# A hybrid encoder block on one core: the first norm applied by diagonal matmuls in a fixed TensorE order, and the mixer's first half in another order

## The chip, the core and the metric

The kernel runs on one core of a Trainium2 chip. A core has TensorE (PE in the profile; its weight loads are PEld), VectorE (DVE), ScalarE (ACT), GpSimd (POOL) and SyncE (SP, which only issues DMAs). The metric is the device time of one execution in microseconds. A comparison takes several runs of both kernels on the same chip; one more execution is recorded by the hardware profiler.

## The reference

x is 1024 tokens by 1024 features, float32. One trunk layer is computed:

```python
x = x + 0.5 * swiglu(rmsnorm(x, ffn1_norm), w_gate1, w_up1, w_down1)   # D_FF = 2816
h = rmsnorm(x, mix_norm); p = h @ w_in
u_a, v_a, qkv, z, b_raw, a_raw = split(p)
y_a = gelu(u_a) * (W_s @ layernorm(gelu(v_a)) + b_s)       # blocks of 128 tokens, 8 groups of 64 channels
q, k, v = split(silu(causal_conv4(qkv)))                   # 4 heads x 128; q, k are l2-normed
beta = sigmoid(b_raw); g = cumsum(-exp(a_log) * softplus(a_raw + dt_bias))   # within chunks of 64
L = strict(beta_i k_i.k_j exp(g_i - g_j))                  # per chunk
u, w = solve(I + L, [beta v, beta k exp(g)])
S, o = scan over the chunks (S: 128 x 128 per head), with attn = tril(q_i.k_j exp(g_i - g_j))
y_b = rmsnorm(o, dn_norm) * silu(z)
x = x + concat(y_a, y_b) @ w_out
x = x + 0.5 * swiglu(rmsnorm(x, ffn2_norm), w_gate2, w_up2, w_down2)
return rmsnorm(x, final_norm)
```

## The kernel before

**Arithmetic.** A large product of f32 data is made of three matmuls in the fp32r type: each operand is split into a high part (a cast by ScalarE) and a low part (a subtraction by VectorE or GpSimd), and `mm3` (L55) adds high x high, high x low and low x high in PSUM. The FFNs use a Winograd form of Strassen's scheme: the activations are cut into four blocks (two token halves by two feature halves), `Combos` holds the transposed blocks B11, B12, B21, B22 and their sums T1 to T4, `load_gu` (L181) makes the matching sums of the weights on GpSimd and splits them. Matmul outputs go to two pools of four PSUM banks, "mm" and "ax".

**Order.** The program is written with a tile framework. A planner puts the instructions of each engine in an order by their place in the program and its own estimate of when they are ready, so the order on an engine can differ from that of the text; at run time each engine goes through its list in order and waits by semaphores. Tiles of one tag share a fixed number of buffers, and a new tile waits until the last user of its buffer is done. DMAs are issued by the SP and ACT queues in their order.

**First FFN's start (`start1`, L467 to L500).** The 8 tiles of x (128 tokens each) arrive by SP; a broadcast copy of the gain (`grow`, L64) arrives by the ACT queue. `normed` (L80) squares and sums a tile on ScalarE, forms the reciprocal root (VectorE L76, then a power on GpSimd, L70), and multiplies x by root and gain on VectorE (L82; L493 for the second four tiles). `Combos.blocks` transposes each tile in 128 x 128 pieces on TensorE (L95), and ScalarE and VectorE evacuate them as split blocks (L118, L119, L141, L142) and as the sums' sources (L137, L148, L150). The first chunk of gate and up is computed plainly, 256 tokens of each half at a time (`gu_plain`, L229): 96 matmuls of 256 columns each time. Then `put_sums` makes T1 to T4, and from chunk 1 on (`gu`) the dense stream runs: 84 matmuls of 512 columns a chunk, while GpSimd and VectorE prepare the next chunk's weights and, every other chunk, the sums for the down product (`weight_sums`, `hidden_sums`).

**Mixer, first half (`middle`).** hT is the normed x, transposed. `token_steps` gives a token-major product, one step per 128 tokens (24 matmuls of 256 columns); `proj_steps` gives a feature-major one, 24 matmuls of 512 columns for each token half, then the convolution (ScalarE copy, four VectorE passes L871 and L873, SiLU on ScalarE L875). In the text the order is:

1. v0 (first half of v), and beside it `decay(h)` (L786) for the four heads: rows of g are broadcast from DRAM, VectorE and GpSimd form g_i - g_j with a mask, ScalarE exponentiates, twice: EL for L, EA for attn.
2. `keys(h, fill)` (L885): the projection of head h's keys, two steps of `fill` (z1, the second half of z), then for both token halves transposes, norms, k's decayed copies, the Gram matmuls in banks "sc" and "sd" and Lm, which goes to DRAM.
3. `substitute()` (L911): the 32 x 32 diagonal blocks of all L are inverted at once, 31 steps of two VectorE passes (L920, L922).
4. `gm_consts`, and v1 (second half of v): GELU, then `mix` (L1074, layernorm on VectorE with a power on GpSimd) and `spatial` (L1088, matmuls with W_s for a pair of tiles, bias added by VectorE).
5. Projections 8 and 0 (v and q of head 0), then per half head: `inverse` (TensorE and copies), `values`, `queries`, woven with the next projections, and `scan`, which walks four chunk pairs through three PSUM banks "sc", "sq", "sd".

## Time and profile before

| what | value |
|---|---|
| median of 3 runs | 1849.43 us (1847.9 to 1852.1) |
| the profiled execution | 1841.22 us |
| its span, first to last instruction | 1839.4 us |
| mean granted TensorE clock | 0.992 |
| from HBM, to HBM | 208.83 MB, 91.77 MB |
| up to the dense stream of the first FFN | 0 to 62.7 us |
| first FFN and z0 | 62.7 to 707 us |
| mixer, v0 to the first inverse | 707 to 893 us |
| mixer, inverse and scan | 893 to 1055 us |
| output projection, second FFN, final norm | 1055 to 1839 us |

How to read it: a row of a timeline is start, duration, engine, line, operation, out<-in by the program's names, shapes and count; in brackets stands the engine's idle time before it and what ended the wait. A row of groups gives count, busy time, mean ns of one, and idle time before. Line numbers are those of the kernel before.

### The profile page before, as it was taken

The page shows a single profiled execution, that of the slowest core. Times are in us where ns is not written, and L with a number is a line of the kernel's source. Part 1 is how long each engine was busy: PE and PEld are TensorE (multiplying, and loading weights), DVE is VectorE, ACT ScalarE, POOL GpSimd, SP SyncE. Part 2 cuts the span into 40 slices and gives each one's busy share as a digit, 9 for nine tenths or more (in the row PEclk, how much of TensorE's full clock was granted, in tenths as well). Part 3 has the DMA queues.
Part 4 walks back from the last instruction along what each step waited for, and adds up shares of the span by engine and source line. Part 5 has one row for each costly group of instructions (what it writes and reads, how often), then busy time and mean ns, then how long its engine had stood idle before and what let it go on. Part 6 is the DMA issues. An engine that isn't in the chain of part 4 may idle for free.

```text
span 1839.4 us, 25484 instructions
## 1 busy us (share of the span) xinstructions
PE 1784.1 (97%) x9735; PEld 1524.8 (83%) x9735; DVE 1191.7 (65%) x1531; ACT 686.6 (37%) x1193; POOL 747.9 (41%) x583
## 2 busy tenths in 40 slices
PE   5999999999999999898999999999999999999997
PEld 4888888888788889797788989988888888878886
DVE  6867676665565575769655344587776766656546
ACT  6333332333343454432344533452333323243433
POOL 4667666565140012212132420366666665614001
PEclk9999999999999999999999999999999999999999
DMA  5353443544957445453432254334535445495744
GB/s 196 108 175 136 162 152 134 184 158 163 339 188 258 155 177 164 140 195 100 133 94 67 90 197 136 109 104 165 178 132 171 144 154 188 142 344 185 264 142 149
DMA packets 134441, 302.26 MB, mean 164 GB/s; under 512 B 27408, under 2 KB 42032, under 8 KB 134320
## 3 DMA queue, kind: packets, MB, share of 16 engines
q1 hardware_dynamic: 131824, 296.20, 46.9%
q10 hardware_dynamic: 2496, 4.44, 0.8%
q8 instruction: 76, 1.25, 0.3%
q14 instruction: 45, 0.37, 0.1%
HBM read 208.83 MB, written 91.77 MB: 163 GB/s over the span
## 4 chain that ended last, share of the span: by engine, by line
PE 78%; DVE 8%; DMA 5%; POOL 4%; issue 3%; ACT 2%; SPq 0%; POOLq 0%; DVEq 0%; ACTq 0%
PE mm L53 43%; PE ax L53 32%; POOL s L191 1%; POOL t L278 1%; DMA left<-hq 1%; DVE acc L873 1%; PE ax L95 1%; PE sd L53 1%; DMA graw<-in_f1gu_dram 1%; POOL s L278 1%; PE sc L53 1%; DVE T L119 0%; DVE unit L62 0%; DVE wk L62 0%; DVE E L797 0%
## 5 line engine op out<-in xcount | busy, mean ns | idle before, releaser
L53 PE MATMUL mm<-unit 128*128 128x512 f32 x1056 | 244.9, 392 | 4.2 <-ACT unit L61 2.2
L53 PEld LDWEIGHTS mm<-unit 128*128 128x128 f32 x1056 | 198.8, 189 | 47.4 <-ACT unit L61 3.3
L191 POOL TENSOR_TENSOR s<-graw 128x512 f32<-128x512 f32 x84 | 130.3, 1551 | 262.9 <-DMA graw<-in_f2gu_dram 116.0
L62 DVE TENSOR_TENSOR ga<-graw,ga 128x512 fp32r<-128x512 f32 x134 | 155.9, 1166 | 99.9 <-ACT ga L61 99.2
L61 ACT CAST gs<-s 128x512 fp32r<-128x512 f32 x168 | 104.5, 622 | 301.8 <-PE mm L53 151.0
L62 DVE TENSOR_TENSOR unit<-left,unit 128x1024 fp32r<-128x1024 f32 x84 | 101.9, 1215 | 133.0 <-ACT unit L61 132.3
L53 PE MATMUL ax<-T,gs 128*128 128x512 f32 x792 | 183.1, 389 | 0.0
L53 PE MATMUL ax<-unit 128*128 128x512 f32 x792 | 180.5, 389 | 0.0
L53 PEld LDWEIGHTS ax<-T,gs 128*128 128x128 f32 x792 | 148.7, 188 | 30.8
L53 PEld LDWEIGHTS ax<-unit 128*128 128x128 f32 x792 | 148.7, 188 | 30.8
L62 DVE TENSOR_TENSOR gs<-s,gs 128x512 fp32r<-128x512 f32 x168 | 172.7, 1030 | 2.3
L53 PE MATMUL mm<-B,ga 128*128 128x512 f32 (+1 forms) x864 | 166.8, 347 | 3.3 <-ACT B L118 1.9
L61 ACT CAST unit<-left 128x1024 fp32r<-128x1024 f32 x84 | 82.5, 982 | 230.2 <-PE ax L53 100.5
L53 PE MATMUL mm<-T,gs 128*128 128x512 f32 x720 | 166.5, 389 | 0.0
L53 PEld LDWEIGHTS mm<-B,ga 128*128 128x128 f32 x864 | 139.5, 194 | 23.4 <-ACT B L118 2.5
L53 PEld LDWEIGHTS mm<-T,gs 128*128 128x128 f32 x720 | 135.2, 188 | 28.0
L70 POOL TENSOR_TENSOR rs<-rs,half 128x1 f32<-128x1 f32 (+1 forms) x29 | 19.2, 662 | 334.5 <-DVE rs L76 334.4
L53 PE MATMUL mm<-actT,wk 128*128 128x512 f32 x576 | 150.4, 403 | 0.0
L53 PE MATMUL ax<-B,ga 128*128 128x512 f32 x528 | 127.2, 390 | 1.4 <-DVE ga L62 1.4
L53 PE MATMUL mm<-wk,actT 128*128 128x256 f32 x960 | 123.5, 285 | 2.7 <-DVE wk L62 2.7
L53 PEld LDWEIGHTS mm<-wk,actT 128*128 128x128 f32 x960 | 117.4, 190 | 3.4 <-DVE wk L62 3.0
L53 PEld LDWEIGHTS mm<-actT,wk 128*128 128x128 f32 x576 | 103.6, 188 | 18.8
(239 smaller groups left out, 3046.0 us busy)
## 6 DMA issues: line engine op xcount, KB each, us to landing
left<-hq SPq DMA_DIRECT2D x70, 512.0 KB, 5.0
graw<-in_f1gu_dram SPq DMA_DIRECT2D x44, 512.0 KB, 5.4
wq<-t SPq DMA_DIRECT2D x44, 512.0 KB, 2.8
hq<-s SPq DMA_DIRECT2D x44, 512.0 KB, 3.1
graw<-in_f2gu_dram SPq DMA_DIRECT2D x44, 512.0 KB, 4.7
right<-wq SPq DMA_DIRECT2D x40, 512.0 KB, 4.8
wd<-in_f1wd_dram SPq DMA_DIRECT2D x22, 512.0 KB, 6.6
hq<-sg SPq DMA_DIRECT2D x22, 512.0 KB, 3.7
```

The lines of the kernel that those rows point to most:

```text
L53: nc.tensor.matmul(*args, **kw)
L61: nc.scalar.copy(h, src)
L62: nc.vector.tensor_tensor(l, src, h, op=ALU.subtract)
L70: nc.gpsimd.tensor_tensor(o, i, half[:, :w], op=ALU.pow)
L95: nc.tensor.transpose(ps[:, i * P:(i + 1) * P], blk(i), ident)
L191: nc.gpsimd.tensor_tensor(f, u, v, op=op)
L278: nc.gpsimd.tensor_tensor(o, u, v, op=op)
L873: nc.vector.scalar_tensor_tensor(acc, pad[:, j:j + 512], cw[:, blk, j:j + 1], acc, op0=ALU.mult, op1=ALU.add)
```

## The change

There are three groups of edits. The first is at the start: the gain arrives as a column layout (`f1g`, 128 x 8) and the norm is no longer applied to x. Instead a diagonal matrix of the tile's reciprocal roots is made (identity times root), and the block's transposition becomes a plain f32 matmul of x with that diagonal; the gain is applied on evacuation, per partition. Tiles 0, 1, 4, 5 come first, then 2, 3, 6, 7; four tiles fill a bank of 512 columns. TensorE's order is fixed by hand there, and begins with 24 matmuls of the identity. `gu_plain` becomes a generator that goes by k over all four accumulators (in both FFNs), woven with the blocks.

```diff
+        def scaled_blocks(self, i, pp, xts, dg, g, f, b12, ahead):
+            sl = slice(i * 256, i * 256 + 256)
+            t3, t1, t2, t4 = self.f[i] = f
+            def less(o, src, c, v):
+                nc.vector.scalar_tensor_tensor(o, src, g[:, c:c + 1], v, op0=ALU.mult, op1=ALU.subtract)
+            def put(h, l, src, c):
+                nc.scalar.mul(h, src, g[:, c:c + 1])
+                less(l, src, c, h)
...
+            def turn(k):
+                cs = range(len(banks), len(banks) + k)
+                banks.extend(bank(*pp) for _ in cs)
+                for n, x in enumerate(xts):
+                    for c in cs:
+                        mm(banks[c][:, n * P:n * P + P], x[:, c * P:c * P + P], dg[:, n * P:n * P + P], start=True, stop=True)
+            turn(ahead)
+            for c in range(8):
+                if c == len(banks):
+                    turn(1)
+                u, v = banks[c][:, :256], banks[c][:, 256:]
+                k = c % 4
+                if c < 4:
+                    b = self.block("B11")
+                    put(b[:, 0, k, sl], b[:, 1, k, sl], u, c)
+                    nc.scalar.mul(t3[:, k], u, g[:, c:c + 1])
+                    b = b12[k // 2]
+                    put(b[:, 0, k % 2], b[:, 1, k % 2], v, c)
+                    less(t1[:, k], v, c, t3[:, k])
+                else:
+                    b = self.block("B21")
+                    put(b[:, 0, k, sl], b[:, 1, k, sl], u, c)
+                    b = self.block("B22")
+                    put(b[:, 0, k, sl], b[:, 1, k, sl], v, c)
+                    less(t2[:, k], v, c, t1[:, k])
+                    less(t4[:, k], u, c, t2[:, k])
+                yield
...
+            def plain(i, dg, fs, b, ahead, also=()):
+                bl = cb.scaled_blocks(i, f.X, [xs[t] for t in order[i]], dg, g1, fs, b, ahead)
+                together(islice(bl, 4))
+                together(also)
+                pr = f.gu_plain(slice(i * 256, i * 256 + 256), b)
+                for _ in bl:
+                    next(pr)
+                together(pr)
+            with tc.manual_schedule(engines={mybir.EngineType.PE}):
+                warm = bank(*f.X)
+                for _ in range(24):
+                    mm(warm[:, :P], ident, ident, start=True, stop=True)
+                weights = f.load_gu(0, True)
+                dg = factors(order[0], nc.vector.tensor_scalar_mul)
+                together(islice(weights, 2))
+                xs.update(load_x(xdram, order[1]))
+                plain(0, dg, four(cb.sums() + cb.sums()), b12(), 4, weights)
+                dg = factors(order[1], nc.scalar.mul)
...
+                plain(1, dg, fs, b12(), 1)
+            together(f.load_gu(1), *(cb.scaled_sums(i, ("T2", "T1", "T3", "T4"), (V, G, V, G)) for i in range(2)))
```

`scaled_sums` is `put_sums` for 256 tokens at a time. The first `weight_sums` moves from chunk 1 to chunk 2. The reciprocal roots of norms, keys and `mix` are formed by two GpSimd instructions (`rsqrt`: add, power) in place of a VectorE and a GpSimd one. At the end of the second FFN the last tile's halves change places, and tile 6's last multiplication is handed back to the caller.

The second group is the decay: only EL stays in `decay`, g_i goes into the exponential as ScalarE's bias (four instructions of 128 columns in place of one of 512), and attn's factor is made in `values`, per half head:

```diff
     def decay(h):
-        EL[h], EA[h] = (xp.tile([P, 2, 512], F32, tag="x", name="E") for _ in range(2))
+        EL[h] = xp.tile([P, 2, 512], F32, tag="x", name="E")
         for hf in range(2):
...
+            rows_of(grb, h * 2 + hf)
+            (nc.vector if hf else nc.gpsimd).tensor_tensor(v4(EL[h][:, hf]), masked(K(C_ML)), v4(grb), op=ALU.subtract)
+            exponents(EL[h][:, hf], gc, h * 2 + hf)
...
             nc.scalar.copy(self.u, up)
+            aT = self.aT = big("aT", 2)
+            rows_of(aT, self.n)
+            nc.vector.tensor_tensor(v4(aT), masked(cma), v4(aT), op=ALU.add)
+            exponents(aT, ngc, self.n)
             yield
```

The third is the order of steps 2 to 5. v1 becomes the filling of the keys, z1 comes after them, TensorE's order is fixed from the keys to the end of z1, and projection 8's VectorE work is queued behind the last substitution step:

```diff
-    fill = token_steps([a["wz1"][0], a["wz1"][1]], 256, spill("z", 1), hT)
-    for h in range(HEADS):
-        keys(h, fill)
-    together(fill)
-    substitute()
     gm = gm_consts()
+    gm_shift(gm)
     later = []
-    tm("v", 1, ev_v(gm, later))
+    fill = steps("v", 1, ev_v(gm, later))
+    PE = mybir.EngineType.PE
+    with tc.manual_schedule(engines={PE}):
+        for h in range(HEADS):
+            keys(h, load_qkv(4 + h), fill)
+        z1 = token_steps([a["wz1"][0], a["wz1"][1]], 256, spill("z", 1, nc.scalar.copy), hT, ahead=True)
+        next(z1)
+        for g in later:
+            g()
+        w8 = load_qkv(8)
+        last = substitute()
+        together(z1)
...
-    proj_conv(8, values_of(0))
-    later.pop()()
+    with tc.issue_after(last.ins):
+        together(proj_steps(8, w8, values_of(0)))
     proj_conv(0, queries_of(0))
```

In `keys` the first token half is worked off before the two filling steps, the second after them. In `mix` the layernorm's scaling becomes one ScalarE pass; its gain is multiplied in when `spatial` evacuates (VectorE), and its shift, W_s's row sums times the bias plus b_s, is precomputed by `gm_shift` (eight matmuls of one column) and added by GpSimd. v1's tiles move from the "kst" buffers to the "x" buffers.

271 lines of the change are left out of this document (147 added, 124 removed).

## The prediction

> **What bounds the kernel now.** First the page: the span, the engines' shares, and the chain that ended last.
>
> ```profile
> span 1839.4 us, 25484 instructions
> PE 1784.1 (97%) x9735; PEld 1524.8 (83%) x9735; DVE 1191.7 (65%) x1531; ACT 686.6 (37%) x1193; POOL 747.9 (41%) x583
> PE 78%; DVE 8%; DMA 5%; POOL 4%; issue 3%; ACT 2%; SPq 0%; POOLq 0%; DVEq 0%; ACTq 0%
> ```
>
> TensorE is the bound, so what matters is where it is idle. The table of busy time by stage (columns: stretch, its length, then each engine's busy time and count) shows it:
>
> ```profile
> 9.00:23.00 14.00, 10.59 (x57) 9.09 (x58) 11.17 (x20) 10.42 (x23) 3.59 (x5) 1.00 0.78 315
> 23.00:62.70 39.70, 29.85 (x204) 27.61 (x202) 35.75 (x41) 25.04 (x49) 28.17 (x20) 0.83 0.22 80
> 62.70:386.00 323.30, 323.30 (x1426) 267.78 (x1427) 235.41 (x243) 100.60 (x169) 207.97 (x132) 1.00 0.45 156
> 713.00:757.00 44.00, 39.00 (x272) 36.58 (x272) 32.74 (x41) 21.24 (x48) 14.05 (x13) 0.96 0.39 124
> 757.00:812.00 55.00, 55.00 (x339) 49.32 (x338) 35.20 (x74) 15.92 (x52) 10.04 (x30) 1.00 0.47 160
> 812.00:890.00 78.00, 72.43 (x454) 64.65 (x452) 67.37 (x157) 23.80 (x52) 15.70 (x22) 1.00 0.51 160
> 950.00:1055.00 105.00, 104.22 (x912) 91.65 (x912) 50.23 (x111) 49.04 (x119) 35.63 (x45) 1.00 0.28 83
> ```
>
> Before 62.7 us, where the first FFN's dense stream begins, TensorE is idle 9.0 (its first row, below, starts at 9.36) + 3.4 + 9.9 = 22.3 us. In the mixer's first half it is idle 5.0 us (713 to 757) and 5.6 us (812 to 890). In the FFN stream and the scan stage (950 to 1055) it hardly waits. The change works on the first two. The TensorE rows of the start, with what ended each wait:
>
> ```profile
> 9.36 1.11 PE L95 MATMUL ax<-ident,x 128*128 128x128 f32 x4 [9.36 <-DVE x L82]
> 36.26 0.63 PE L95 MATMUL ax<-ident,x 128*128 128x128 f32 x4 [3.56 <-DVE x L493]
> 38.47 2.79 PE L95 MATMUL ax<-ident,x 128*128 128x128 f32 x12 [1.58 <-DVE x L493]
> 62.67 1.66 PE L53 MATMUL ax<-B,ga 128*128 128x512 f32 x6 [1.42 <-DVE ga L62]
> ```
>
> The releaser is VectorE each time: it multiplies whole rows of x by norm and gain (L82, L493), and is behind with everything else.
>
> **The start, part by part.** Prices on TensorE come from a stretch without waits (start, duration):
>
> ```profile
> 809.73 2.16 PE L53 MATMUL mm<-wk,actT 128*128 128x256 f32 x17
> 811.73 0.60 PE L844 MATMUL ax<-ident,kst 128*128 128x128 f32 x4
> 812.17 1.06 PE L53 MATMUL sc<-kst 128*128 128x128 f32 x8
> 813.06 0.60 PE L844 MATMUL ax<-ident,kst 128*128 128x128 f32 x4
> ```
>
> From start to start a 256-wide product takes 2.00/17 = 0.118 us, a transpose 0.44/4 = 0.11, and one record of a plain f32 matmul 0.89/8 = 0.11. L844's four transposes are four records; the four Gram matmuls (sc) are eight. So a matmul against a diagonal costs two records where a transpose cost one: 64 blocks of x give 128 records, 14.1 us in place of 7.0. The products stay: 2 x 96 x 0.118 = 22.7 us. The 24 warming matmuls are 48 records. They need only the identity, which I put at 4.6 us, when the first x is in (ACT row below). At first a record takes 1.11/4 = 0.28 us (the 9.36 row). I let 16 pass so and 32 at 0.11: 8.0 us, to 12.6.
>
> [...]
>
> When can the diagonals be there?
>
> ```profile
> 4.56 1.06 ACT L74 ACTIVATE f<-x 128x1024 f32<-128x1024 f32 x1 [1.64 <-DMA x<-in_x_dram]
> 11.03 1.04 ACT L74 ACTIVATE f<-x 128x1024 f32<-128x1024 f32 x1
> 5.97 0.56 POOL L70 TENSOR_TENSOR rs<-rs,half 128x1 f32<-128x1 f32 x1 [5.55 <-DVE rs L76]
> ```
>
> Now the fourth square starts at 11.03 behind the broadcast gain, which goes (a 128x8 load replaces it). I put it at 9 and its diagonal, after 1.2 of square, 0.8 on GpSimd and 0.3 on VectorE, at 11.5. So the warming decides, not the norm. TensorE then needs 12.6 + 14.1 + 22.7 = 49.4, plus 1.8 for the first evacuation (the fifth block's turn needs the first bank back: three VectorE passes of 0.42 and one ScalarE pass ahead), so it reaches the dense stream at 51.2.
>
> VectorE has its own sum. Its groups up to 62.7 us:
>
> ```profile
> L119 DVE TENSOR_TENSOR T<-f,T 128x512 fp32r<-128x512 f32 x8 | 10.6, 1380 | 0.0
> L493 DVE SCALAR_TENSOR_TENSOR x<-x,rs,grow 128x1024 f32<-128x1024 f32 x4 | 6.9, 1777 | 3.5 <-POOL rs L70 3.5
> L62 DVE TENSOR_TENSOR ga<-graw,ga 128x512 fp32r<-128x512 f32 x5 | 6.1, 1241 | 0.0
> L82 DVE SCALAR_TENSOR_TENSOR x<-x,rs,grow 128x1024 f32<-128x1024 f32 x4 | 5.0, 1283 | 3.4 <-DMA grow<-in_ffn_norm_dram 2.1 <-POOL rs L70 1.3
> L142 DVE TENSOR_TENSOR B<-ax,B 128x256 fp32r<-128x256 f32 x8 | 3.2, 417 | 0.8 <-ACT B L141 0.7
> ```
>
> L82 and L493 (11.9 us) go. The new blocks take 28 VectorE passes of 256 columns a half; 56 x 0.417 = 23.4. The T sums (10.6), weight splits (6.1) and SwiGLU products (4 x 0.42) stay. That is 42 us, of which some 4 (the first splits) pass before 16 us, when the first bank is full. 16 + 38 = 54. Two sums, 51 and 54; I take 54, as the rows say that VectorE is what ended the waits. **Start: 62.7 - 54 = 8.7 us won.** Bounds: 11.5 (TensorE's sum alone) and 0 (the fixed order waits at each bank as the old one did at each row). The first wd sums moved past chunk 1 are four GpSimd passes and four DMA issues; the stream hides them (GpSimd 208 of 323 us busy).
>
> **The mixer's first half.** Its waits:
>
> ```profile
> 745.78 5.92 PE L53 MATMUL mm<-wk,actT 128*128 128x256 f32 x35 [2.75 <-DVE wk L62]
> 755.52 0.66 PE L844 MATMUL ax<-ident,kst 128*128 128x128 f32 x4 [2.25 <-ACT kst L875]
> 840.48 2.02 PE L53 MATMUL ax<-vm,u 128*128 128x128 f32 x16 [2.89 <-DVE vm L1084]
> L802 DVE TENSOR_TENSOR E<-E,csa 128x512 f32<-128x512 f32 x8 | 8.1, 1014 | 0.0
> L797 DVE TENSOR_TENSOR E<-grb,gc 128x512 f32<-128x512 f32 x8 | 8.0, 1030 | 5.0 <-DMA grb<-grd 5.0
> ```
>
> The first two come from decay(): VectorE builds both exponentials there. L797 and L802 (16.1 us) leave, so I count these 5.0 us as won. The third comes from mix() standing on VectorE between substitution steps. With v1 filling the keys, mix has slack, and z1, evacuated by ScalarE, runs beside the substitution: 5.6 won. What is late next: the last key half holds one of two "ax" banks while four spatial() calls, fixed behind it, want two; I charge 2. [...] v1 among the keys brings there, on ScalarE, GELUs, eight normalizations and two table switches a head (8 x 1.28 = 10.3 us); from 757 to 812 it is busy 15.9 of 55 us, and a key half's convolution has the other half's 24 matmuls (5.5 us) over it, so I take that at nothing; if that cover fails it costs a switch a head, 5 us. On SP the loads of v's first half come between the key stores; Ld's last store stays last.
>
> Does the substitution end in time?
>
> ```profile
> L920 DVE TENSOR_TENSOR aT<-Lb,X x31: 191/359/419, 831.0 to 882.4; 128x31 f32<-128x31 f32 x2, 128x60 f32<-128x60 f32 x2, 128x87 f32<-128x87 f32 x2, 128x112 f32<-128x112 f32 x2
> 893.16 0.41 PE L53 MATMUL ax<-Z,L 32*32 32x32 f32 x8 [1.17 <-DMA Z<-xz]
> ```
>
> 62 passes of 0.34 (a little under the median) are 21 us, now spread over 52. The keys' last matmuls end near 814.4 (the transposes at 813.06 and eight records more), Lb lands 17 us later, and the first inverse starts 10.5 us after the last step. That makes 17 + 21 + 10.5 = 48.5 us. Over it lie spatial 4 x 2.0, z1 192 x 0.118 = 22.7 and two projections of 48 matmuls at 323.3/1426 = 0.227 (21.8): 52 us. Covered by 4. The wait that issue_after adds holds projection 8's convolution, and its "mm" bank, behind the last pass, 38 us after the keys; projection 8's first half ends after 2 + 8 + 22.7 + 5.5 = 38 us, so nobody waits long. **Won: 5.0 + 5.6 - 2 - 1 = 7.6, say 8 us**; bounds 10.6 and 2.
>
> **The scan stage.** Eight masked adds of VectorE, eight row loads of SP and 32 exponentials of ScalarE move here, out of decay(). Behind a load that waits for its aT buffer stand the next inverse's loads on SP. Exp and Silu need different tables:
>
> ```profile
> 716.15 1.28 ACT L775 ACT_TABLE_LOAD   x1
> 745.67 1.28 ACT L875 ACT_TABLE_LOAD   x1
> L1118 ACT ACT_TABLE_LOAD x3 | 3.8, 1283 | 0.1
> L1034 ACT ACT_TABLE_LOAD x2 | 2.6, 1283 | 0.0
> 1033.19 1.28 ACT L1118 ACT_TABLE_LOAD   x1
> 1034.48 0.38 ACT L1118 ACTIVATE ev<-mm 128x256 f32<-128x256 f32 x1
> L1027 ACT ACTIVATE oh<-sq,ex 128x128 f32<-128x128 f32 x31 | 11.4, 368 | 16.4 <-PE sq L53 16.0
> ```
>
> The first two rows are the switch to Exp and on to Silu; the next two are all loads from 890 to 1055. Eight halves make 16 switches, 16 x 1.28 = 20.5 us, and 32 x 0.37 = 11.8 us of exponentials. TensorE waits for ScalarE copies in inverse() and for the read of the "sq" bank. The old kernel makes five loads there, all at the end, and TensorE idles 0.8 us from 950 to 1055: 0.16 a load at most, 2.6 us for 16. **Lost: 3 us**; bounds 0 and 32.
>
> [...]
>
> **The rest: 0.** The gate/up order by k in the second FFN (bounds 1 won, 2 lost: all four banks end at once, covered by the next half's transposes), the reciprocal roots on GpSimd (one short pass for another), and the last tile's halves.
>
> **The sum.** 8.7 + 8 - 3 = 13.7 us. The profiled execution took 1841.2 us (span 1839.4), so it gives 1827.5. The median of three runs stands 8.2 higher, 1849.4; I take the same difference there: 1835.7. Within 0.2%, 3.7 us, a measurement can't tell this kernel from no change.
>
> **The rivals.**
> *A, the waits move.* VectorE and fixed banks bound the start, as the 38 us above already leave it nothing spare: the start wins 3, the mixer 5, and the scan loses 3, so 1844. For it: beside GpSimd's work L493 took 1.78 us for the shape that takes L82 1.28, so the T passes (1.38) may grow too. Against it: 12 us of VectorE's work are gone.
> *B, slower: ScalarE's switches stand in the scan.* Planned order does not move at run time, so a copy of inverse() behind a load and four exponentials comes 1.28 + 1.5 us late, and Silu's load follows. It decides once over half of the 32.3 us falls through to TensorE (16.7/32.3). At three quarters it is 24.2 - 16.7 = 7.5 lost: 1857. Against it stand the five loads and their 0.8 us.
> *C, not as it says.* Only TensorE's order is fixed; if the planner still spreads the substitution over 52 us, the first inverse comes 52 - 21 - 4 = 27 us late, of which 48 matmuls of the next projection (11 us) can be drawn ahead: 16 lost, 1835.7 + 16 = 1852. Against it: no mix is left to weave in.
>
> **How the numbers follow.** Forecast 0.60, all faster. A 0.22: 0.17 faster, 0.05 same. B 0.11: 0.10 slower, 0.01 same. C 0.07: 0.02 same, 0.04 slower, 0.01 faster. Faster 0.78, same 0.08, slower 0.14. The range goes from all upper bounds won (11.5 + 10.6 + 1 = 23: 1826, and 2 for the short gaps that busy time hides: 1824) to 1851, which holds A and leaves out C and B; about 0.2 lies outside.
>
> **What would show it.** First dense stream product near 54 us, with no wait on x rows before it; TensorE idle under 4 us between 713 and the end of z1; the substitution's 62 passes within 24 us; 16 more table loads after it, with idle there up by about 3. It is wrong if the stream starts after 60, or if TensorE's idle time in the scan grows by over 10.

## The result and the profile after

The changed kernel takes 1864.4 us (median of 4 runs, 1859.3 to 1866.5) against 1848.7 us of the kernel before (1847.9 to 1852.1) on the same chip: a ratio of 1.0076, 95% interval 1.0056 to 1.0096 (below, intervals stand behind their ratios). It is 16 us slower, where 13.7 us faster was forecast. The profiled execution took 1866.5 us, close to its median; that of before took 1841.2 us, 7.5 under its own. So the two traces stand 25 us apart, of which 9.6 are that chance (7.5 and 2.1). Line numbers from here on are those of each run's own kernel.

The head of the page after:

```profile
span 1864.7 us, 25872 instructions
PE 1811.0 (97%) x9863; PEld 1548.7 (83%) x9863; DVE 1117.8 (60%) x1468; ACT 767.1 (41%) x1322; POOL 758.1 (41%) x639
```

TensorE's share is the same 97%, although it has only some 14 us more to do in the text (128 records of the diagonals for 64 transposes, 48 of warming, 16 of gm_shift). Its busy time grew by 27 us, and the mean granted clock of the span fell from 0.992 to 0.983. A busy time that grows more than the work was here the first hint of a lower clock.

Three TensorE rows stand at the same place of both programs: the first product of the first FFN's down stage, the output projection's first long run, and the first down product of the second FFN. Before:

```profile
464.33 0.50 PE L53 MATMUL mm<-unit 128*128 128x512 f32 x1 [1.97 <-ACT unit L61]
1089.49 5.78 PE L53 MATMUL mm<-wo,actT 128*128 128x256 f32 x46 [2.52 <-DVE wo L62]
1618.36 0.50 PE L53 MATMUL mm<-unit 128*128 128x512 f32 x1 [0.23 <-ACT unit L61]
```

After:

```profile
465.93 0.49 PE L53 MATMUL mm<-unit 128*128 128x512 f32 x1 [1.88 <-ACT unit L61]
1104.56 5.71 PE L53 MATMUL mm<-wo,actT 128*128 128x256 f32 x33 [2.51 <-DVE wo L62]
1640.63 0.49 PE L53 MATMUL mm<-unit 128*128 128x512 f32 x1 [1.41 <-ACT unit L61]
```

From row to row the kernel after falls behind by 1.6 us (start and first FFN), 13.5 (mixer), 7.2 (output projection and the second FFN's first half) and 3.0 (the rest). Nothing is won anywhere. The table of busy time by stage (stretch, length, then busy time of PE, PEld, DVE, ACT and POOL, and after them the granted clock) shows the mixer's part:

```profile
710.00:757.00 47.00, 45.17 (x341) 42.79 (x340) 19.14 (x34) 34.96 (x82) 10.84 (x21) 1.00 0.52 175
757.00:812.00 55.00, 54.74 (x331) 48.01 (x330) 35.42 (x68) 35.26 (x84) 19.83 (x50) 1.00 0.38 129
812.00:831.00 19.00, 12.78 (x93) 12.05 (x92) 13.74 (x25) 8.06 (x17) 12.85 (x20) 0.91 0.70 256
831.00:880.00 49.00, 49.00 (x326) 44.34 (x325) 32.94 (x80) 15.93 (x26) 5.05 (x7) 1.00 0.55 151
880.00:886.00 6.00, 1.80 (x22) 1.24 (x20) 5.86 (x8) 5.31 (x10) 0.31 (x1) 0.81 0.73 231
886.00:908.00 22.00, 22.00 (x122) 16.29 (x121) 5.20 (x13) 3.67 (x8) 0.28 (x2) 0.51 0.13 34
908.00:1070.00 162.00, 160.72 (x1372) 138.53 (x1371) 88.67 (x183) 111.57 (x226) 53.68 (x64) 1.00 0.30 89
```

The 5.0 us beside decay() fell to 1.8, and the 5.6 us beside the substitution to 0 (831 to 880). But 6.2 us stand at the end of the keys (812 to 831) and 4.2 at the first inverse (880 to 886). Idle time up to the scan is 12.5 us, where it was 11.7. Then comes a row that has no counterpart before: from 886 to 908 TensorE is never idle and its clock is 0.51. Those 22 us did the work of 11.

The last row is the scan, with its sixteen new switches to Exp: TensorE is idle 1.3 us in 162 there, in the kernel before 1.1 in 161 (894 to 1055).

**Two parts of every time.** Each run comes with its span and its mean granted clock, so span x (1 - clock) is what the lower clock took, and the remainder is the time at full clock, waits included. The split is rough, since half clock costs nothing while TensorE has nothing to do: in the profile before, the clock is 0.50 from 1832.2 us to the end, 7.2 us, and TensorE is not busy there at all. Means over the runs (one run of the kernel before, of 3601.7 us, is left out as slow):

| kernel | runs | median us | ratio to before, 95% | lost to the clock | remainder |
|---|---|---|---|---|---|
| before (all its runs) | 162 | 1847.1 | 1 | 20.6 | 1825.5 |
| changed | 4 | 1864.4 | 1.0076 (1.0056 to 1.0096) | 28.9 | 1833.0 |
| E1 no Exp in the scan | 9 | 1870.3 | 1.0101 (1.0074 to 1.0128) | 27.4 | 1840.2 |
| E2 copies on VectorE | 10 | 1863.3 | 1.0070 (1.0040 to 1.0101) | 30.2 | 1832.8 |
| E3 junk under the wait | 10 | 1865.6 | 1.0082 (1.0057 to 1.0107) | 25.3 | 1838.1 |
| E4 second FFN by product | 10 | 1858.9 | 1.0028 (1.0000 to 1.0056) | 24.7 | 1832.7 |
| E5 = E4 + sums late | 12 | 1855.9 | 1.0050 (1.0032 to 1.0068) | 21.5 | 1832.2 |
| E6 = E4 + old start | 12 | 1857.7 | 1.0054 (1.0032 to 1.0077) | 27.4 | 1828.3 |
| E7 = E4 + z1 between | 12 | 1852.9 | 1.0030 (1.0012 to 1.0049) | 20.0 | 1830.4 |
| E8 = E5 + E7 + Lb first | 12 | 1852.1 | 1.0034 (1.0014 to 1.0054) | 21.8 | 1829.2 |
| E9 = changed + dense run | 11 | 1858.3 | 1.0051 (1.0028 to 1.0074) | 22.8 | 1833.5 |
| E10 = E8 + two inverses | 11 | 1847.3 | 0.9996 (0.9978 to 1.0015) | 17.5 | 1828.2 |
| E11 = E10 + old start | 12 | 1848.0 | 0.9982 (0.9957 to 1.0007) | 19.2 | 1826.6 |
| E12 = E10, T3 late only | 11 | 1844.0 | 0.9984 (0.9965 to 1.0002) | 16.2 | 1825.6 |
| E13 = E12 + more ahead | 9 | 1841.4 | 0.9962 (0.9946 to 0.9978) | 14.1 | 1824.2 |
| E14 new start, old mixer | 12 | 1850.6 | 1.0026 (1.0007 to 1.0045) | 17.6 | 1831.4 |
| E15 = E13 + old start | 12 | 1844.6 | 0.9976 (0.9954 to 0.9997) | 20.0 | 1822.6 |
| E16 = E13 + add on VectorE | 6 | 1836.2 | 0.9940 (0.9917 to 0.9963) | 15.6 | 1818.8 |
| E17 = changed + add on VectorE | 6 | 1856.4 | 1.0052 (1.0033 to 1.0071) | 23.8 | 1829.8 |
| E18 = changed, three undone | 12 | 1848.3 | 1.0011 (0.9997 to 1.0024) | 19.1 | 1827.5 |

Of the 16 us, some 8 are clock and 8 are waits and work. The mean clock is printed to three places, so one run's loss is known to 0.9 us, a mean over ten runs to about 0.3. Differences of one or two us in the ratio are within the intervals. The runs were made on several chips and at several times. From one set of runs to the next the kernel before had medians of 1845.4 to 1849.7 us, a loss to the clock of 19.0 to 22.9 and a remainder of 1824.8 to 1825.8. So remainders carry best from one row to another, and then ratios; a comparison of medians or losses between rows is good to 2 to 4 us only.

### The profile page after: what moved, and what is told of

It is laid out like the page before. It is cut to its first block, busy times and chain, and to the rows that moved or that the text cites. A ratio compares the mean times of both kernels' runs of the same rounds, so it can differ in the third digit from the quotient of the medians.

```text
span 1864.7 us, 25872 instructions
## 1 busy us (share of the span) xinstructions
PE 1811.0 (97%) x9863; PEld 1548.7 (83%) x9863; DVE 1117.8 (60%) x1468; ACT 767.1 (41%) x1322; POOL 758.1 (41%) x639
## 5 line engine op out<-in xcount | busy, mean ns | idle before, releaser
L62 DVE TENSOR_TENSOR ga<-graw,ga 128x512 fp32r<-128x512 f32 x134 | 133.8, 1001 | 122.2 <-ACT ga L61 121.7
L53 PE MATMUL mm<-actT,wk 128*128 128x512 f32 x576 | 157.0, 414 | 0.0
L74 POOL TENSOR_SCALAR rs<-ms 128x1 f32<-128x1 f32 x23 | 12.4, 539 | 316.7 <-ACT xn L79 136.3
L53 PEld LDWEIGHTS ax<-B,ga 128*128 128x128 f32 x528 | 99.0, 188 | 20.5
```

Of the source, the lines that this page charges most:

```text
L53: nc.tensor.matmul(*args, **kw)
L62: nc.vector.tensor_tensor(l, src, h, op=ALU.subtract)
L74: nc.gpsimd.tensor_scalar(o, i, add, None, op0=ALU.add)
```

## The experiments

The first theory (S in the expectations) was read from the first inverse. TensorE's rows there, in the changed kernel:

```profile
876.74 0.59 PE L53 MATMUL ax<-Z,L 32*32 32x32 f32 x16
877.26 3.69 PE L53 MATMUL mm<-actT,wk 128*128 128x512 f32 x15
885.15 0.91 PE L53 MATMUL ax<-rv,X 32*32 32x32 f32 x16 [4.20 <-ACT rv L1054]
885.99 1.65 PE L53 MATMUL mm<-actT,wk 128*128 128x512 f32 x3
```

And ScalarE's at the same time (its table loads and the copy that TensorE waits for):

```profile
875.18 1.28 ACT L886 ACT_TABLE_LOAD   x1 [1.67 <-DMA aT<-grd]
876.89 1.28 ACT L966 ACT_TABLE_LOAD   x1
879.31 1.28 ACT L886 ACT_TABLE_LOAD   x1
883.03 1.28 ACT L966 ACT_TABLE_LOAD   x1
884.86 0.52 ACT L1054 COPY rv<-ax 32x128 f32<-32x128 f32 x2
```

The first inverse's product is done at 877.3, and its copy starts at 884.86, behind four exponentials of two halves and projection 0's copies and SiLUs. So ScalarE's switches looked like the cause.

**E1, the decay kept in DRAM.** In the text, beside the masked rows for L:

```diff
+            nc.vector.tensor_tensor(v4(grb), masked(cma), v4(grb), op=ALU.add)
+            exponents(grb, ngc, h * 2 + hf)
+            nc.sync.dma_start(ead[h * 2 + hf], grb)
...
-            rows_of(aT, self.n)
-            nc.vector.tensor_tensor(v4(aT), masked(cma), v4(aT), op=ALU.add)
-            exponents(aT, ngc, self.n)
+            nc.sync.dma_start(aT, ead[self.n])
```

> The changed kernel, with attn's decay factor made beside the keys as before and kept in DRAM: the step that makes the rows for L also adds the mask and exponentiates for attn and stores 256 KB a half, and values() loads that instead of making it. So no Exp stands in the scan. Theory S (in the trace of the changed kernel, ScalarE reaches the copy that the first inverse waits for 7.6 us after its product, behind four table loads and four exponentials; TensorE is idle 4.2 us and then runs at a granted clock of 0.50 for some 22 us, worth about 11): 15 us faster than the changed kernel, near 1849, and no stretch at 0.50 after the first inverse. Rival M (the mixer lost its time to the late keys and the late substitution, and the first inverse would wait for its DMAs anyway): at most 4 us faster. Rival F (the second FFN's start, gate and up by k, is the loss): within 2 us of the changed kernel.

It came out slower still, 1.0101. The wait at the first inverse shrank to 2.5 us, and the clock lost 1.7 us there instead of 11.9; but the exponentials now stand among the keys. E1's table of busy time, for its keys and spatial():

```profile
713.00:848.00 135.00, 120.98 (x795) 110.44 (x794) 72.42 (x135) 86.44 (x213) 47.50 (x92) 0.95 0.50 168
```

TensorE is idle 14.0 us there, against 8.3 in the changed kernel from 710 to 831. So theory S was right that the place is dear (1.7 us of wait and 10.2 of clock went), and its remedy was not: what was won there was lost among the keys.

**E2, the copies on VectorE.**

```diff
-                nc.scalar.copy(Pm[B32[i], :P], pp[B32[i], :P])
+                nc.vector.tensor_copy(Pm[B32[i], :P], pp[B32[i], :P])
```

(and the 64-row copy likewise)

> The changed kernel, with the three copies in inverse() that make its left factors put on VectorE in place of ScalarE; the exponentials and all table loads stay. Theory S (ScalarE's order at the first inverse): the same gain as without any Exp in the scan, 13 us, though ScalarE has as many loads as in the changed kernel. Rival B as predicted (each of the 16 switches costs its 1.3 us somewhere in the scan): at most 4 us faster, since the values and queries still wait for ScalarE. Rival M: at most 4 us.

Nothing won. The TensorE row of the wait in E2, and VectorE's rows ahead of it:

```profile
884.94 0.63 PE L53 MATMUL ax<-rv,X 32*32 32x32 f32 x8 [3.88 <-DVE rv L1054]
```

```profile
881.45 0.49 DVE L962 TENSOR_SCALAR acc<-pad,cw 128x512 f32<-128x512 f32 x1 [2.57 <-ACT pad L960]
881.97 2.33 DVE L964 SCALAR_TENSOR_TENSOR acc<-pad,cw,acc 128x512 f32<-128x512 f32 x3
884.61 0.27 DVE L1054 COPY rv<-ax 32x128 f32<-32x128 f32 x1
```

The copy now stands behind projection 0's convolution, which itself waits for ScalarE. So theory S falls as it was put: it is not the engine that is slow, but the planned order, in which projection 0 goes ahead of the inverse on every engine that serves both. TensorE has to be given something to do for those 8 us.

**E3, junk under the wait.**

```diff
+            if self.n == 0:
+                yield
+                jb = bank(ps_s, "sq")
+                for _ in range(24):
+                    tc.keep_in_program_order(nc.tensor.matmul(jb, hT[0][0][:, 0, 0, :P], hT[0][0][:, 0, 0], start=True, stop=True))
```

> The changed kernel, with 24 matmuls of 512 columns into an unused bank (their result is not read) between the first inverse's first product and the wait for its copy: 24 x 0.227 = 5.4 us of extra work in a wait of 4.2 us that stays as it is. Theory S with the clock as the larger part: TensorE is never idle for over 1 us there, the granted clock stays at 1.00, and the kernel is 9 us faster though it does more. Rival: the clock's share is nothing (the 22 us at 0.50 cost nothing, or the clock falls anyway): 1 us slower.

In E3's trace the wait is down to 0.7 us and no stretch under full clock follows it: the 11.9 us of clock lost there are gone. But the forecast, 9 us faster, missed, and the time is the rival's, 1 us slower. Over ten runs the clock loses only 3.6 us less than in the changed kernel, and the remainder is 5.1 more, which is the junk (5.4). In E3's trace three other stretches at half clock, at 468, 823 and 1099 us, are each 3.4 us longer than in the changed kernel's (1.7 lost each). So the trace shows the mechanism at its place; the total doesn't show that it is worth 11.9 us.

**E4, the second FFN product by product.** The old loop of gu_plain, for the second FFN alone:

```diff
-        def gu_plain(sl, b12):
+        def gu_plain(sl, b12, by_k=True):
...
+            for i, x in () if by_k else ((0, "B11"), (1, "B12"), (0, "B21"), (1, "B22")):
+                first = x[1] == "1"
+                for p, wt in ((gates[i], g["B11" if first else "a12"]), (ups[i], g["a21" if first else "a22"])):
+                    products(p, wt, xs[x], sl, first, not first)
...
-            together(f.gu_plain(slice(0, 256), b))
+            together(f.gu_plain(slice(0, 256), b, False))
...
-            together(f.gu_plain(slice(256, 512), c))
+            together(f.gu_plain(slice(256, 512), c, False))
```

> The changed kernel, with the plain gate and up of the second FFN in the old order (product by product, all eight k of a product in turn); the first FFN keeps the order by k. Theory: in the changed kernel TensorE waits 2.2 and 1.1 us there for the up weights' split and for x, and the clock falls to 0.50 for 7 us (3.5 lost): with the old order 4 to 6 us faster than the changed kernel. Rival: VectorE and the residual additions bound that place, not the order: within 1 us.

As expected: 5.5 us by the medians (1.0028 against 1.0076; the intervals just touch). By the table 4.2 of it is clock and 0.3 remainder. TensorE at the second FFN's start in the changed kernel:

```profile
1201.60 1.00 PE L53 MATMUL mm<-B,ga 128*128 128x256 f32 x5
1204.80 2.08 PE L53 MATMUL mm<-B,ga 128*128 128x256 f32 x8 [2.20 <-DVE ga L62]
1207.99 11.72 PE L53 MATMUL mm<-B,ga 128*128 128x256 f32 x83 [1.11 <-DVE x L676]
```

And in E4:

```profile
1205.01 2.90 PE L53 MATMUL mm<-B,ga 128*128 128x256 f32 x22 [1.37 <-DVE ga L62]
1208.20 7.46 PE L53 MATMUL mm<-B,ga 128*128 128x256 f32 x60 [0.29 <-DVE x L680]
```

By k, the sixth product already needs the second half of the weights (up), whose split comes 2.2 us later; product by product the twelve gate products run first. The eight products at 1204.80 take 0.26 us each at a granted clock of 0.50 (from 1204.7 to 1206.9), where such a product takes 0.118 in the prediction's stretch without waits, at a clock of 1.00.

**E5, the first half's sums behind the last block.** Here is the wait of 7 us at the start, in the changed kernel. TensorE:

```profile
46.35 2.05 PE L53 MATMUL ax<-dg,x 128*128 128x128 f32 x8 [6.83 <-DVE f L167]
63.57 2.91 PE L53 MATMUL ax<-B,ga 128*128 128x512 f32 x12
```

GpSimd, ScalarE and VectorE ahead of it:

```profile
36.98 3.32 POOL L210 TENSOR_TENSOR f<-f 128x1024 f32<-128x1024 f32 x1
```

```profile
40.34 1.05 ACT L212 CAST T<-f 128x1024 fp32r<-128x1024 f32 x1 [2.20 <-POOL f L210]
```

```profile
41.42 2.28 DVE L213 TENSOR_TENSOR T<-f,T 128x1024 fp32r<-128x1024 f32 x1 [2.82 <-ACT T L212]
43.95 0.86 DVE L167 SCALAR_TENSOR_TENSOR B<-ax,ba,B 128x256 fp32r<-128x256 f32 x2
```

T3 of the first half goes GpSimd, ScalarE, VectorE, and each engine waits for the one before. The planner put all three ahead of the second half's evacuations, for which TensorE waits. E5 queues them behind:

```diff
+                with tc.issue_after(cb.last.ins), tc.issue_after(cb.cast.ins):
+                    next(ss[0])
```

> E4's kernel (second FFN product by product), and at the start the sums T1 to T4 of the first half are queued on VectorE and ScalarE behind the last block of the second half. In the changed kernel TensorE waits 7.0 us for the first bank of the second half, while VectorE waits 2.8 us, in its order, for a sum that ScalarE casts behind a GpSimd pass of 3.3 us; the clock then falls to 0.50 (3.4 us lost). Theory Q (an order of VectorE and ScalarE that puts early sums ahead of the evacuations makes the wait): the dense stream starts at 55 to 58 us instead of 63.6 and the kernel is 4 to 8 us faster than E4. Rival K (the sums are due then anyway): the stream starts near 56, but waits 5 us or more for T2 to T4; within 2 us of E4.

The dense stream starts at 54.7 us, but then waits for what was put off (E5, TensorE):

```profile
54.73 2.91 PE L53 MATMUL ax<-B,ga 128*128 128x512 f32 x12
58.39 0.50 PE L53 MATMUL ax<-T,gs 128*128 128x512 f32 x1 [0.53 <-DVE T L213]
60.07 7.11 PE L53 MATMUL ax<-T,gs 128*128 128x512 f32 x23 [1.17 <-DVE gs L62]
```

E4's stream starts at 64.1. Of the 9.4 us that E5's starts earlier, 2.9 are left at the down stage; there the first product waits for a cast whose weights a DMA brings, in either kernel. The ratio (1.0050) can't be told from E4's. Rival K came nearer, though the waits of the stream are some 2 us by these rows and not 5.

**E6, the mixer alone.** E4 with the start of the kernel before; start1's core goes back to:

```diff
-                dg = factors(order[0], nc.vector.tensor_scalar_mul)
-                together(islice(weights, 2))
-                xs.update(load_x(xdram, order[1]))
-                plain(0, dg, four(cb.sums() + cb.sums()), b12(), 4, weights)
...
+            parts = [cb.blocks(i, f.X, xi(i), uv[i], b) for i in range(2)]
+            together(*parts, n=2)
+            together(*parts, weights)
```

> E4's kernel with the start of the kernel before (gain as rows, VectorE multiplies x, transposes, gate and up product by product, planner's order, the first weight sums in chunk 1): so of the change only the mixer's new order, the decay in the scan, and the reciprocal roots and the last tile are left. Theory: the new start costs 2 to 4 us (in E4 the first FFN's end comes 3.7 us later than in the kernel before, in the changed kernel 1.6), so this is 2 to 4 us faster than E4, and still 5 us slower than the kernel before, by the mixer. Rival, as predicted: the new start wins 8.7 us, so this is that much slower than E4.

1.0054, not to be told from E4 and E5. So the new start is worth nothing that these runs could show, either way: its remainder is 4 us more, its loss to the clock 3 to 6 us less. And the mixer with the small edits alone makes the kernel 0.5% slower.

**E7 and E8, the keys' tail and Lb.** One step of z1 ahead of each spatial(); in E8 also E5's edit, and the load of Lb issued ahead of the stores of spatial():

```diff
         for g in later:
-            g()
+            together(islice(z1, 1))
+            stores.append(g())
         w8 = load_qkv(8)
-        last = substitute()
+        last, first = substitute()
+        with tc.issue_after(first.ins):
+            for s in stores:
+                s()
```

> E4's kernel, with one step of z1 (24 matmuls, 2.8 us) ahead of each of the four spatial() calls on TensorE, in place of all after them. Theory Q: the last keys hold one ax bank until GpSimd's roots and two VectorE passes are done (TensorE waits 0.8 + 3.9 + 1.4 us there and runs 1.7 us' worth at half clock); with z1 under it 6 to 8 us faster than E4. Rival C2 (the first inverse is bound by the substitution, which starts when Lb comes at 841 and ends at 869, and TensorE only arrives there earlier): what is won at the keys is waited for at the first inverse, within 2 us of E4.

> E5 and E7 together, and SP issues the load of Lb ahead of the four stores of spatial(), which stand ahead of it in the changed kernel (9.8 us of SP's queue, so Lb is issued at 835.3 where the last block of L was stored at 823.5). Theory Q: Lb lands near 831, the substitution ends near 858, and all gains add: 12 to 18 us faster than E4, so 1841 to 1847, a little under the kernel before. Rival C2 without the Lb part would hold the mixer where it is: 5 us faster than E4. Rival K: 5 us less.

1.0030 and 1.0034: by the ratio neither can be told from E4; their remainders are 2.3 and 3.5 us less. In E7 the tail's waits fall to 3.0 us, and TensorE then waits 4.4 us at the first inverse for the DMA of Z. In E8 the load of Lb is issued at 827.7 and the substitution ends at 865 us, 7 sooner than in E7. TensorE waits 2.5 us for the copy again, and the clock loses 10 us behind it. Rival C2: what is won at the keys is, for the most part, waited for at the first inverse. One thing differed: in E7 the clock came back after 6.8 us, in E8 after 20.5. E7 has eleven dense products in a row behind the wait, E8 groups of three and four. Theory G takes that difference for the cause. E9 tests it on the changed kernel: if it holds, 4 to 9 us are won by the medians, if not, at most 2.

**E9, a dense run behind the wait.** The changed kernel, with TensorE's order there written by hand:

```diff
-    together(weave(prep, proj_steps(9, wv, values_of(1)), (1,) * 14))
+    with tc.manual_schedule(engines={PE}):
+        together(weave(prep, proj_steps(9, wv, values_of(1)), (0, 3, 5, 1, 1, 0, 1, 1, 1, 1, 0, 1, 0, 1)))
```

> The changed kernel itself, with TensorE's order fixed by hand from the first inverse to the first queries: 9 dense matmuls (of projection 9) ahead of the wait for the first inverse's copy in place of 18, and 15 in a row right behind it in place of groups of three between narrow products. Nothing is taken away, and the wait itself gets no shorter (idle 4 to 6 us). [...]

Median 1858.3, 6 us under the changed kernel, as theory G has it (the intervals of the ratios overlap); the loss to the clock is 22.8 instead of 28.9, and the remainder is unchanged. E9's TensorE rows:

```profile
882.46 0.92 PE L53 MATMUL ax<-rv,X 32*32 32x32 f32 x16 [2.42 <-ACT rv L1054]
883.30 6.26 PE L53 MATMUL mm<-actT,wk 128*128 128x512 f32 x15
889.49 0.43 PE L53 MATMUL ax<-ident,Z 32*32 32x32 f32 x8
890.46 0.97 PE L53 MATMUL mm<-actT,wk 128*128 128x512 f32 x3
```

The fifteen products in a row take 0.42 us each, where the fifteen at 877.26 in the changed kernel took 0.25: the granted clock is 0.50 in E9 from 884 to 888 us, and 1.00 in the changed kernel from 877.3 to 881. The three at 890.46 take 0.97 us together, at 1.00 again. In the changed kernel the three at 885.99 take 1.65 at 0.50, and so do all such groups up to 906. The wait was shorter here too (2.4 us, not the 4 to 6 expected), so this pair alone would not carry theory G. The other traces do: the stretch at half clock at the first inverse is 3.4 or 6.8 us where 8 to 15 products in a row stand in it or follow (E1, E7, E9, E17, E18), and 10.2 (E4), 20.5 (E8), 23.9 (changed, E6), 27.3 (E5) and 30.7 (E2) where groups of three to five stand between narrow products. E4 shows that the groups don't forbid the return: with the changed kernel's order and a wait of 3.9 us its clock was back after 10.2.

**E10 and E11, both inverses together.** E8 with the steps of the two halves paired and 18 dense products between the first and the second pair; E11 has the old start as well.

```diff
+    def pairs():
+        for _ in range(5):
+            next(i0)
+            next(i1)
+            yield
+    prep = chain(pairs(), H[0][0].values(), H[0][0].queries())
+    with tc.manual_schedule(engines={PE}):
+        together(weave(prep, proj_steps(9, wv, values_of(1)), (0, 6, 2, 2, 2, 1, 1, 1, 1)))
```

> E8's kernel, with the two halves' inverses of head 0 step by step together and TensorE's order fixed by hand there: both first products, 18 dense matmuls (4.1 us, as long as the copy took to come), both second products, then 6 dense matmuls between steps. Theory G: no wait over 1.5 us at the first inverse, no stretch at 0.50 there (10 us lost in E8's profile), 6 to 10 us faster than E8 (1852), so 1842 to 1846 and at or under the kernel before. Rival (waits are conserved: the last chain through the substitution sets the end): the wait comes back at the values or the scan's first step, within 3 us of E8.

> E10's kernel with the start of the kernel before. From E4, E5 and E6 (start old against new: the time at full clock 4 us less, the clock's loss 3 to 6 us more): within 3 us of E10. If the new start is worth its first stream's 6 us after all, 4 to 6 us slower than E10; if the old is better by the work it does not add, 4 us faster.

E10 stands at 0.9996, E11 at 0.9982: level with the kernel before. E10 is 4.8 us under E8, nearly all of it clock (21.8 to 17.5). So the first inverse and the clock behind it carry much of the mixer's loss.

**E12 and E13, T3 alone late, and more work ahead of the inverse.** E12 pins only T3 behind the last block and puts a second step of z1 ahead of the first spatial(). E13 also changes the counts of the dense products between the steps (the last two lines of the diff, against E12):

```diff
+                if n == 2:
+                    with tc.issue_after(cb.last.ins), tc.issue_after(cb.cast.ins):
+                        next(ss[0])
+                else:
+                    next(ss[0])
...
         next(z1)
+        together(islice(z1, 1))
         for g in later:
...
-        together(weave(prep, proj_steps(9, wv, values_of(1)), (0, 6, 2, 2, 2, 1, 1, 1, 1)))
+        together(weave(prep, proj_steps(9, wv, values_of(1)), (7, 4, 1, 1, 1, 0, 1, 0, 1)))
```

> E10's kernel, with only T3's cast and subtraction of the first half queued behind the last block (T1, T2 and T4 stay where the planner puts them), and two steps of z1 ahead of the first spatial() in place of one. In E10's trace the stream starts at 55 us but waits 0.7 + 1.5 + 2.2 us for T sums and a weight split at 58 to 68 us, and 3.2 us at the second spatial(). Theory Q: T3 alone made the 7 us wait of the changed kernel, so the stream still starts at 55 to 57 and its later waits fall from 4.3 to under 2.5 us; the wait at the spatial() goes too, with the half clock behind it (1.7): 4 to 7 us faster than E10 (1847), so 1840 to 1843, clearly under the kernel before. Rival (VectorE and GpSimd have no time left for the sums: they are late wherever they stand; and the first inverse waits for the substitution, which ends no sooner): within 2 us of E10.

> E12's kernel with seven steps of projection 9 (21 dense matmuls, 4.8 us) ahead of the first inverse in place of none, and four instead of six behind its first product. In E12 TensorE stands 6.1 us before the first inverse: the substitution's last pass ends at 858.9, the last load of Z lands near 871, and TensorE is there at 862.3. Theory C2 (with the other waits gone the first inverse is bound by the chain keys, L, substitution, Z, and what TensorE can be given under it): the wait falls from 6.1 to 1 to 2 us, the half clock there (5.1 lost) to 1.7 or none, and the kernel is 3 to 6 us faster than E12 (1844), so 1838 to 1841, under the kernel before (1845 to 1849) by over 0.2%. Rival (conserved waits): the steps taken from the inverses leave waits between their products, and it is within 2 us of E12.

E12 won 3 us (0.9984, not to be told from E10 or the kernel before), less than hoped, because the wait moved again. TensorE at the first inverse in E12, and then in E13:

```profile
868.27 0.60 PE L53 MATMUL ax<-Z,L 32*32 32x32 f32 x8 [5.95 <-DVE acc L978]
```

```profile
870.21 0.41 PE L53 MATMUL ax<-Z,L 32*32 32x32 f32 x8 [0.84 <-DMA Z<-xz]
872.71 0.41 PE L53 MATMUL ax<-Z,L 32*32 32x32 f32 x8 [1.17 <-DMA Z<-xz]
```

The inverse starts within 2 us of the same time in the two (Z comes when it comes), but E13 has done 21 products more. E13 stands at 0.9962 (0.9946 to 0.9978): clearly faster than the kernel before.

**E14 and E15, start and mixer apart.** E14 is E12's start with the mixer of the kernel before, E15 is E13's mixer with the start of the kernel before (E6's edit in E13). In E14 the core of keys() goes back, here against the changed kernel:

```diff
-        together(proj_steps(4 + h, w, [k[:, 0] for k in kst]))
-        key_half(h, 0, kst[0])
-        together(islice(fill, 2))
-        key_half(h, 1, kst[1])
+        proj_conv(4 + h, [k[:, 0] for k in kst])
+        for _ in range(2):
+            next(fill, None)
+        for hf in range(2):
```

> The new start (with T3 alone late, as in E12) in front of the mixer of the kernel before: decay, keys, substitution, spatial() and the first projections all as before; the second FFN product by product. So what is left of the change is the start, the reciprocal roots and the last tile. If the start is worth what E12's stream shows (the gs products of the down stage 2 to 4 us earlier, and 5 us of clock), 3 to 6 us faster than the kernel before. If the mixer's new order, in its best form, carried the rest of E12's gain, this is slower than E12 by that; theory Q (the old mixer's waits of 11.8 us were short ones that cost little clock): within 3 us of E12, so that the reordered mixer is worth nothing net of its waits.

> E13's kernel with the start of the kernel before. If the new start (T3 late) is worth 2 to 4 us, as the trace of E12 shows up to the down stage, 2 to 4 us slower than E13 (0.996 of the kernel before), so at 0.997 to 0.999. If E14 is slower than the kernel before because of the new start, 4 us faster than E13, at 0.994. Within 2 us of E13: the start is worth nothing either way, and E14's loss is the small edits'.

E14 is slower than the kernel before (1.0026), by 9 us behind E13. So the mixer's new order, with its waits covered, is worth some 9 us. E15 (0.9976, 3 us behind E13 by the medians) can't be told from E13, so a gain of the start, with T3 late, is not shown: in E13 the clock loses 5.9 us less, and the remainder is 1.6 more. E14 keeps the small edits that the next runs try; as E15 doesn't show its start to cost anything, they are the likeliest cause of its loss.

**E16, E17 and E18, the reciprocal roots.** One line of rsqrt, in E13 (E16) and in the changed kernel (E17); E18 has E17's, E4's and E9's edits.

```diff
     def rsqrt(o, i, add, w=1):
-        nc.gpsimd.tensor_scalar(o, i, add, None, op0=ALU.add)
+        nc.vector.tensor_scalar(o, i, add, None, op0=ALU.add)
```

> E13's kernel with the addition ahead of each reciprocal root on VectorE again in place of GpSimd (the power stays on GpSimd). In E13's trace TensorE waits 0.7 us twice at the first tiles of the mixer's norm and 1.0 and 0.9 us at the second FFN's norms, and in E14 some 3 us more than in the kernel before from the output projection to the second FFN's down stage. If these come from GpSimd's two instructions in a row, 2 to 4 us faster than E13. If the addition costs the same on either, as predicted, within 1.5 us.

> The changed kernel with nothing undone but the addition ahead of each reciprocal root, on VectorE in place of GpSimd. If E16's 5 us are that edit's own price, 5 us faster than the changed kernel, near 1859 (1.005 to 1.006 of the kernel before). If E16 won because the best mixer left it room that the changed kernel has not, within 2 us of it (1.007 to 1.008).

> The changed kernel with three small things undone or mended together: the addition on VectorE (E17), the second FFN product by product (E4), the dense run behind the wait at the first inverse (E9). The start, the keys' order and the wait itself stay. If the three prices add (5 + 5.5 + 6), 16 us faster than the changed kernel, level with the kernel before (0.999 to 1.001). If they overlap (the later waits absorb what an earlier one gives), 8 to 11 us, 1.003 to 1.004.

E16 is the fastest kernel of all, 0.9940 (0.9917 to 0.9963), 11 us under the kernel before, and the version to keep. Against E13 its remainder is 5.4 us less. The group of these additions in the changed kernel, and in E16:

```profile
L74 POOL TENSOR_SCALAR rs<-ms 128x1 f32<-128x1 f32 x23 | 12.4, 539 | 316.7 <-ACT xn L79 136.3 <-ACT o L79 120.6 <-ACT f L79 59.3
```

```profile
L74 DVE TENSOR_SCALAR rs<-ms 128x1 f32<-128x1 f32 x23 | 3.5, 150 | 11.8 <-ACT xn L79 6.8 <-ACT o L79 3.7 <-ACT f L79 1.2
```

The same addition of 128 numbers takes 0.54 us on GpSimd and 0.15 on VectorE. It stands in the chain from a tile's square to its scaled rows, for which TensorE waits at each norm. E17 won 8 us by the median; 3.2 of them are remainder, and the rest is clock: in its trace eight dense products happen to follow the wait at the first inverse, and the clock is back after 6.8 us, as in E9. E18 stands at 1.0011 (0.9997 to 1.0024): the three small edits explain 12 of the 16 us. Singly they had won 8.1, 5.5 and 6.2 by the medians, 20 in all; E17 and E9 mend the same clock, so they don't add. The 4 us that are left are not taken apart by a run.

## Why the prediction was wrong

**The start, 8.7 us expected, about nothing measured.** Two steps failed. The sum "16 + 38 = 54" took VectorE as always at work on what TensorE needs next; in the planner's order it waited 2.8 us for T3, and the stream began at 63.6, 0.9 later than before and so just under the lower bound given. With the early sums behind, it started at 54.7 (E5), which meets the 54 by luck in part: the 38 us hold 10.6 of T sums, of which E5 had done 3.1 by then, and VectorE was busy only 30.5 of the 38.7 us from 16 to 54.7. And the sum ended at the start of the stream: it asked what comes earlier, and not whether the T sums that the stream needs next come earlier too. They don't (E5), and the down stage waits for its weights in either kernel.

**The mixer's first half, 8 us expected, 13.5 lost in the trace up to the output projection.** The three waits did go (5.0 and 5.6 us to 1.8 and 0). "What is late next" was charged 2 us and came to 6.2 at the keys' tail: the key half holds an ax bank as said, and ScalarE and GpSimd serve mix() and the key norms in turn, so TensorE waits for both:

```profile
822.54 6.63 PE L53 MATMUL ax<-vm,u 128*128 128x128 f32 x40 [3.91 <-DVE kst L991]
```

No run shows the 1 us charged for gm_shift; in the trace after its 16 records run from 733.82 to 735.52, 1.7 us, 0.11 each. "Covered by 4" failed twice over. Lb was issued at 835.3, behind four stores of spatial() on SP's queue, 12 us after the last block of L was stored; the prediction had looked at Ld's last store and not at Lb's load:

```profile
823.46 0.37 SPq L996 DMA_DIRECT2D Ld<-aT  x1
825.41 9.76 SPq L1210 DMA_DIRECT2D spm<-vm  x4
835.27 0.42 SPq L1007 DMA_DIRECT2D Lb<-Ld  x1
```

The passes then took from 841.7 to 868.9 us, 27 in place of 24. That alone would have been covered: TensorE reached the first inverse at 876.7, and Z was there. What was late was a copy that the sum did not hold, behind projection 0 on ScalarE. The new order has its worth in the end, for E13 against E14 is 9 us, but only with TensorE's order of the first inverses written anew.

**The clock, no term at all.** The prediction has slow products in the warming alone (0.28 us a record); nothing in it says that a wait costs more than its length. Here the clock is 8 us of the 16 (28.9 lost against 20.6), and in the trace the largest piece, 11.9, followed one wait of 4.2 us.

**The scan, 3 us expected.** TensorE idles 1.3 us in 162, before 1.1 in 161: nothing, the lower bound. The sixteen switches to Exp, thirteen of them in that stretch, cost nothing where TensorE has other work. Rival B had the right mechanism in one place only, the first inverse, and not the scan.

**The rest, 0 expected.** Two of the three dismissals were wrong; the third, the last tile's halves, was not tried alone. The order by k costs 5.5 us in the second FFN (bound given: 2), most of it clock, as its weights are split just in time there. "One short pass for another" costs 3 to 5 us, since this short pass takes 0.54 us on GpSimd and 0.15 on VectorE.

**The rivals.** In mechanism A came nearest (the waits move) and still had the wrong sign, as it priced a moved wait at its own length. B had the right sign and the nearest time, 1857, for a place that cost nothing, the scan: that is luck.

## What to carry to other kernels

Ask of every wait that goes where the same chain is waited for next, engine by engine and queue by queue, down to the last load; here the chain keys, L, Lb, substitution, Z, copy had three such places. A wait on TensorE is worth its length plus the clock behind it (0 to 15.4 us here, the most in E2), so put unbroken wide products after the waits that can't be avoided, and narrow ones later (the stretch at half clock was 6.8 us so in E9, 23.9 in the changed kernel). Price each short instruction that changes its engine from a row of that engine, above all where a chain from tile to tile runs through it.

## What the hardware did that was not expected

In the traces of before and after the granted clock reads 1.00 or 0.50 and nothing between, and all times at which it changes lie whole multiples of 3.41 us apart, as on a grid. Its stretches at 0.50 last 3.41, 6.83, 13.65 and 23.89 us (but for the one at the end of each trace, 9.24 and 6.77), and in the traces of the experiments, but for the end, 3.4 to 30.7; so the losses there are 1.7, 3.4, 5.1, 6.8, 10.2, 11.9, 13.6 and 15.4. Two waits of 2.5 us, ahead of the output projection's run (the second row of the first two blocks of rows above, before and after), show that the length of a wait alone did not decide. Here are steps of the grid, with the columns of the table by stage (the clock is the third figure from the end), first in the kernel before:

```profile
1084.70:1088.11 3.41, 2.14 (x15) 1.31 (x13) 3.22 (x6) 3.41 (x8) 0.00 (x0) 1.00 1.02 382
1088.11:1091.52 3.41, 2.03 (x17) 2.03 (x18) 3.41 (x7) 1.43 (x3) 0.00 (x0) 1.00 0.95 356
```

And the kernel after:

```profile
1102.21:1105.62 3.41, 1.06 (x9) 1.07 (x10) 3.41 (x6) 2.33 (x5) 0.00 (x0) 1.00 0.96 345
1105.62:1109.03 3.41, 3.41 (x19) 3.41 (x18) 2.49 (x5) 0.59 (x1) 0.00 (x0) 0.50 1.01 398
```

Before, the wait is shared by two steps, TensorE is busy for 2.14 and 2.03 us of them, and the clock stays at 1.00. After, one step holds the wait, TensorE is busy for 1.06 us of it, and the next step is at 0.50. Of all the steps at full clock in these two traces, the eleven with 0 to 1.41 us of work were followed by half clock; of six with 1.50 to 1.80, four were; and none with 1.87 or more. So the place of a wait on the grid counted beside its length, and these edits don't set that place: it is chance.

For the way back, what counts is read from the products of the full array (128*128 in the rows). In the same two traces, thirteen steps at half clock with 2.86 to 3.41 us of such products were followed by full clock, and the steps with 2.68 or less by half clock again. In the kernel after, five steps from 887.2 to 904.2 lie within the row from 886 to 908, busy 22.00 of 22.00 at a clock of 0.51: TensorE was busy for all 3.41 us of each, but only 1.9 to 2.7 of them with products of the full array, the others having 32 or 64 rows, and the clock stayed at 0.50. The step behind them had 2.86, and at 907.65 the clock was back. These figures are read from the traces of this kernel alone, where the ends of matmuls are modelled.
